# Splitting two query heads at once and moving 64-row blocks by DMA in a two-layer hybrid decoder step

## The chip, the cores and the metric

The kernel runs on one core of one Trainium2 chip. The metric is the device time of one execution in microseconds (us). A core has a matrix engine (TensorE, PE in the profile; its weight loads are shown apart as PEld), a vector engine (VectorE, DVE), an activation engine (ScalarE, ACT), a general engine (GpSimd, POOL) and SyncE (SP), whose queue issues all the transfers (DMAs) of this kernel. Each engine works through its own list of instructions in order and waits on semaphores for the others. Working data lies in SBUF (128 rows), results of matmuls in PSUM, inputs and outputs in device memory (DRAM).

## What is computed

One inference step over two layers with shared weights: 512 prompt tokens and 8 sample tokens (one for each of 8 sequences), 520 columns in all. Layer 1 is a gated linear recurrence with 16 heads of 128 (HGRN2). From the stream after it, one set of keys and values with 4 heads of 64 is made. Layer 2, the one that this change touches, is sliding-window attention with 32 query heads of 64, eight to a key head, and a sink logit for each head:

```python
HEAD_DIM = 64; N_Q_HEADS = 32; KV_HEADS = 4; WINDOW = 128; SEQ = 512; D_MODEL = 1024
kv = rmsnorm(h, kv_norm_g) @ w_kv
k_sh, v_sh = split(kv)
k_sh = rope_partial(k_sh.reshape(B, L, KV_HEADS, HEAD_DIM), pos)      # first 16 of 64 rotated
q, z = split(xn @ w_in_b)
q = rope_partial(q.reshape(B, L, N_Q_HEADS, HEAD_DIM), pos)
# in blocks of 128 queries, against the block before and their own:
s = einsum('bqhgd,bkhd->bhgqk', q, k) * HEAD_DIM ** -0.5
s = where(in_band, s, -inf)
pr = softmax(concat([s, sink]))[..., :-1]
o = einsum('bhgqk,bkhd->bqhgd', pr, v)
mix = (o.reshape(B, L, 2048) * silu(z)) @ w_out_b
h = h + rmsnorm(mix, post_norm_g); h = h + (p @ w_pe) * sigmoid(h @ w_pg)
```

## The kernel before

All activations lie transposed: 128 features in the rows, 520 tokens in the columns. Each operand of a matmul is split into a high part `hi`, a copy in the type `F32R`, and a low part `lo`, the rest. A projection tile (`Tile128`) is 128 output features: 8 chunks of the 1024 inputs, three products each (`hi*hi`, `lo*hi`, `hi*lo`), two halves of 260 columns, so 48 matmuls `pj<-xs,...` into a pair of PSUM banks. Weights come in transfers of 512 KB (`wr`, two buffers); ACT makes their high part `wh`, DVE or POOL the low part `wl` (four pieces of each are kept ahead).

Layer 2 has eight units (0 to 7) of four query heads. A unit is two query tiles, each with two heads of 64 rows, and two gate tiles. `query(c)` takes a query tile out of PSUM: `rope` is four vector operations (`tmp<-pj,ropeC`, a shuffle `tmp<-pj`, `tmp<-tmp,ropeS`, `tmp<-tmp,tmp`), and then for each of the two heads ACT writes the scaled high part into the head's 64 rows of a new tile `g`, and DVE the low part into the other 64 rows of the same tile. With 64 rows of high part above 64 rows of low part (or the other way round), one matmul over 128 rows does both products with a key tile that holds the same 64 rows twice. `keys_values` makes these key tiles `Kh` and `Kl` (in the profile `xr<-x`): the key's two parts are split once over 128 rows (`x`), and each head's 64 rows are then copied twice, `Kh` by ACT and `Kl` by DVE. The scores are the matmuls `ph<-xr,g`.

After that `block` runs once for each 128 queries of a unit: ACT copies the scores out (`b<-ph`), DVE puts the mask in (`b<-pmask,...`), takes the minimum (`an<-b`), ACT does four exponentials, one operation multiplies by the reciprocal (`b<-b,ad`), PE transposes (`ph<-ident,b`), ACT and DVE split the result (`g<-ph`, `g<-ph,g`), two multiplications mask it (`g<-g,tmask`), and PE applies the values (`ph<-g,b`, 512 columns). DVE adds the halves (`ao<-ph,m`), and at the unit's end multiplies by the gate and splits (`og`). `sample_b` does the attention of the sample tokens once for every four units; it clears its query tile `qs` with a POOL memset.

The output projection runs in groups: after unit 3's projections that of units 0 and 1, after unit 5's that of units 2 and 3, and so on (`GROUPS_B`).

The order of the instructions is not that of the code. Every operation is first only recorded by `Plan.enter`, with its dependencies and a cost from `price`. `Plan.issue` then goes through a modelled time and gives each engine what can start first; on PE, work beside the projections (attention) goes ahead of the next projection matmul as soon as it is ready. Operations recorded with `nc.either` go to DVE or, where DVE would not get to them soon, to POOL: `wl`, `b<-b,ad` and `g<-g,tmask` are such. Since all are issued by one helper, nearly every row of the profile has the line L164, and one goes by tiles' names. What comes out is a fixed order for each engine, with semaphores; the chip does not reorder it. The cost of a transfer in that model:

```python
t = max(t, lanes[0])
clock[e] = t + 0.45
pipe = max(pipe, t + 1.4) + cost       # cost: bytes / 3.3e5 us
op.end = pipe + 1.6
```

The functions that the diff touches, and what calls them:

Of the kernel before, what the change touches and what calls it, by code (L numbers as in the profile page):

```python
# [9 lines left out]
F32 = mybir.dt.float32  # L10
F32R = mybir.dt.float32r
I32 = mybir.dt.int32
AF = mybir.ActivationFunctionType
ALU = mybir.AluOpType
# [7 lines left out]
SEQ = 512  # L22
# [6 lines left out]
HD = 64  # L29
EPS = 1e-6  # L30
SCALE = HD ** -0.5
# [351 lines left out]
def half_of(x, half):  # L383
    return x[:, half * TH : (half + 1) * TH]


class Step:
# [647 lines left out]
    def keys_values(self, kvx):  # L1035
        nc = self.nc
        self.ks = [self.cp.tile([P, NB], F32, name=f"ks{n}") for n in range(2)]
        self.vs = self.cp.tile([NB, KVH * HD], F32, name="vs")

        def first():  # L1040
            if not self.Kh:
                self.Kh = [self.xr_(F32R, SEQ) for n in range(KVH)]
                self.Kl = [self.xr_(F32R, SEQ) for n in range(KVH)]

        def key(j):
            def evac(ps):
                k = self.x_()
                self.rope(ps, self.CR, self.SR, k)
                first()
                nc.sync.dma_start(self.o["ck"][j], k[:, SEQ - P : SEQ])  # L1050
                nc.sync.dma_start(self.o["ck_s"][j], k[:, SEQ:])
                nc.scalar.copy(self.ks[j], k[:, SEQ:])
                self.beside(lambda: twice(j, k))
            return evac

        def twice(j, k):
            hi, lo = self.split(k, self.x_)
            for a in range(2):
                n = 2 * j + a
                src = slice(a * HD, (a + 1) * HD)  # L1060
                for b in range(2):
                    dst = slice(b * HD, (b + 1) * HD)
                    nc.scalar.copy(self.Kh[n][dst], hi[src, :SEQ].bitcast(F32))
                    nc.vector.tensor_copy(self.Kl[n][dst], lo[src, :SEQ].bitcast(F32))

        def value(j):
            def evac(ps):
                v = self.x_()
                for h in range(2):
                    nc.vector.tensor_tensor(half_of(v, h), ps[:, h, :TH], half_of(self.R, h), op=ALU.mult)  # L1070
                if j == 0:
                    V = [self.small("b4", [P, 2, KVH, 2 * HD], 5, F32R) for n in range(2)]
                    self.V = [v[:, n] for v in V for n in range(2)] + [self.small("b2", [P, KVH, 2 * HD], 3, F32R)]
                pt = self.bank()
                for c in range(NCH):
                    nc.tensor.transpose(pt[:, c * P : (c + 1) * P], v[:, c * P : (c + 1) * P], self.ident)
                vt = self.tmp_(cols=SEQ)
                nc.scalar.copy(vt, pt)
                nc.sync.dma_start(self.o["cv"][:, j * P : (j + 1) * P], vt[:, SEQ - P :])
                rows = lambda c: vt[:, c * P : (c + 1) * P]  # L1080
                ds = self.tmp_(cols=3 * P)
                for n, c in ((0, 0), (2, 2), (1, 1), (3, 1), (4, 3)):
                    x = rows(c)
                    if n % 2 or n == 4:
                        d = ds[:, n // 2 * P : (n // 2 + 1) * P]
                        nc.either.tensor_tensor(d, x, rows(0 if n == 1 else 2), op=ALU.subtract)
                        x = d
                    x = x.rearrange("p (n d) -> p n d", n=2)
                    V = self.V[n][:, 2 * j : 2 * j + 2]
                    nc.scalar.copy(V[:, :, :HD], x)  # L1090
                    nc.either.tensor_tensor(V[:, :, HD:], x, V[:, :, :HD].bitcast(F32), op=ALU.subtract)
                p8 = self.bank()
                nc.tensor.transpose(p8[:NB, :P], v[:, SEQ:], self.ident)
                nc.scalar.copy(self.vs[:, j * P : (j + 1) * P], p8[:NB, :P])
                if j == 1:
                    nc.sync.dma_start(self.o["cv_s"], self.vs)
            return evac

        evs = ((2, value(0)), (3, value(1)), (0, key(0)), (1, key(1)))
        return [Tile128([(Weights(self.i["w_kv"][n]), 0)], KC, kvx, ev) for n, ev in evs]  # L1100

    def unit_proj(self, u, xs, st, done):

        nc = self.nc
        kvh = u // 2
        rows = slice((kvh % 2) * HD, (kvh % 2 + 1) * HD)
        st["Q"], st["z"], st["og"] = [], [], []

        def query(c):
            def evac(ps):  # L1110
                q = self.tmp_()
                self.rope(ps, self.C, self.S, q)
                for a in range(2):
                    s = self.g_(F32R)
                    me = slice(a * HD, (a + 1) * HD)
                    other = slice((1 - a) * HD, (2 - a) * HD)

                    nc.scalar.activation(s[me, :SEQ], q[me, :SEQ], AF.Copy, scale=-SCALE)
                    nc.vector.scalar_tensor_tensor(
                        s[other, :SEQ], q[me, :SEQ], -SCALE, s[me, :SEQ].bitcast(F32), op0=ALU.mult, op1=ALU.subtract  # L1120
                    )
                    st["Q"].append(s)
                    nc.scalar.copy(self.qs[rows, :, u % 4 * 4 + 2 * c + a], q[me, SEQ:])
                if c == 1 and u % 4 == 3:
                    self.beside(lambda: self.sample_b(u // 4), FIRST)
            return evac

        def gate(c):
            def evac(ps):
                t = self.tmp_()  # L1130
                nc.scalar.activation(self.two(t), self.flat(ps), AF.Tanh, scale=0.5)
                z = self.g_()
                nc.vector.scalar_tensor_tensor(
                    self.two(z), self.two(t), 1.0, self.flat(ps), op0=ALU.add, op1=ALU.mult
                )
                st["z"].append(z)
                if c == 0:
                    st["zs"] = self.small("zb", [P, 2, NB], 6)
                nc.scalar.copy(st["zs"][:, c], z[:, SEQ:])
                if c == 1:  # L1140
                    done()
            return evac

        def before():
            if u % 4 == 0:
                self.qs = self.small("qs", [P, NB, 16], 1)
                nc.gpsimd.memset(self.qs, 0.0)

        w = lambda n: [(Weights(self.i["w_in_b"][n]), 0)]
        return [Tile128(w(2 * u + c), KC, xs, query(c), before if c == 0 else None) for c in range(2)] + [  # L1150
            Tile128(w(16 + 2 * u + c), KC, xs, gate(c)) for c in range(2)
        ]
# [477 lines left out]
```

## Time and profile before

| | |
|---|---|
| Median of 3 runs | 1095.58 us (1094.31 to 1096.26) |
| The profiled execution | 1095.56 us, of which its span 1093.8 us |
| TensorE clock granted | 0.999 |
| PE / PEld / DVE / ACT / POOL busy | 98% / 97% / 85% / 64% / 11% of the span |
| DMA | 159.37 MB, 146 GB/s on average |

The span is the time from the first instruction to the last; the 1.8 us between it and the execution's time lie around it. Times in the rows below are us from the span's start, unless marked ns. A group's row ends in: busy time, mean ns of one | idle time of the engine just before them, and what ended it. A matmul's row is longer than the distance to the next, because matmuls are pipelined. The keys and values are projected in the stretch up to about 675 us, the eight units' projections with their attention and the output projection run from there to about 1030 us, and the rest is the residual, the norm and the per-layer gate.

### The profile page before, as it was taken

The numbers are of one execution on the slowest core, as the hardware profiler recorded it, in microseconds if no ns is written. First come the engines' busy times: TensorE is split into PE (matmuls) and PEld (weight loads), VectorE is DVE, ScalarE is ACT, GpSimd is POOL, SyncE is SP. The second block draws the span as 40 slices with busy tenths as digits, with TensorE's granted clock in tenths as the row PEclk, the third lists the DMA queues.
The fourth block names the chain that finished last, engine by engine and source line by source line (L and its number), as shares of the span: only waits on it lengthen the run. The fifth ranks groups of instructions, "written<-read, shape, count | busy, mean of one in ns | idle before, by whom it ended". The sixth has DMA issues, their size and how long they took to land.

```text
span 1093.8 us, 23692 instructions
## 1 busy us (share of the span) xinstructions
PE 1073.2 (98%) x8831; PEld 1058.5 (97%) x8831; DVE 924.3 (85%) x1986; ACT 700.9 (64%) x1849; POOL 125.4 (11%) x209
## 2 busy tenths in 40 slices
PE   7999999999999999999999999999999999999998
PEld 6999999999999999999999999999999999999998
DVE  7898888758789588888879989999986997999883
ACT  7787667557775576777636656776674773774551
POOL 1211121011220112121101000111110000000000
PEclk9999999999999999999999999999999999999999
DMA  8555767556666566677655442221213122214433
GB/s 275 174 194 170 195 178 210 147 170 211 168 202 177 154 203 191 194 204 212 200 156 172 133 144 83 75 86 59 83 54 96 59 78 97 78 62 147 144 102 93
DMA packets 148427, 159.37 MB, mean 146 GB/s; under 512 B 100308, under 2 KB 107356, under 8 KB 148312
## 3 DMA queue, kind: packets, MB, share of 16 engines
q1 hardware_dynamic: 148312, 157.85, 47.5%
q8 instruction: 70, 1.15, 0.4%
q14 instruction: 45, 0.37, 0.1%
HBM read 130.03 MB, written 27.78 MB: 144 GB/s over the span
## 4 chain that ended last, share of the span: by engine, by line
PE 72%; DVE 13%; DMA 5%; ACT 5%; issue 3%; SPq 2%; POOL 0%; POOLq 0%; DVEq 0%; ACTq 0%
PE pj L164 59%; PE ph L164 13%; DVE tmp L164 3%; DVE g L164 2%; SPq L164 2%; DMA xr<-td 2%; DVE wl L164 2%; DVE b L164 1%; DVE ao L164 1%; DVE xr L164 1%; ACT b L164 1%; DVE acc L164 1%; ACT g L164 1%; DVE og L164 1%; ACT wh L164 1%
## 5 line engine op out<-in xcount | busy, mean ns | idle before, releaser
L164 PE MATMUL pj<-xs,wh 128*128 128x260 f32 x3328 | 569.4, 285 | 0.9 <-ACT xs L164 0.7
L164 PEld LDWEIGHTS pj<-xs,wh 128*128 128x128 f32 x3328 | 469.4, 189 | 4.4 <-ACT xs L164 1.9
L164 PE MATMUL pj<-xs,wl 128*128 128x260 f32 x1664 | 348.2, 285 | 0.0
L164 PEld LDWEIGHTS pj<-xs,wl 128*128 128x128 f32 x1664 | 260.7, 188 | 0.6
L164 ACT CAST wh<-wr 128x512 fp32r<-128x512 f32 x288 | 177.3, 619 | 121.8 <-PE pj L164 110.4
L164 DVE TENSOR_TENSOR wl<-wr,wh 128x512 fp32r<-128x512 f32 x274 | 187.7, 688 | 54.0 <-ACT wh L164 53.4
L164 PE MATMUL pj<-og,wh 128*128 128x260 f32 x1056 | 184.9, 285 | 0.7 <-ACT g L164 0.5
L164 PEld LDWEIGHTS pj<-og,wh 128*128 128x128 f32 x1056 | 151.6, 188 | 2.5 <-ACT g L164 0.7
L164 PE MATMUL pj<-og,wl 128*128 128x260 f32 x512 | 107.9, 285 | 0.0
L164 ACT ACTIVATE tmp<-pj 128x520 f32<-128x520 f32 (+1 forms) x93 | 48.0, 528 | 53.9 <-PE pj L164 53.4
L164 PEld LDWEIGHTS pj<-og,wl 128*128 128x128 f32 x512 | 80.9, 189 | 0.5
L164 ACT ACTIVATE sb<-sb,g 128x128 f32<-128x128 f32 x128 | 65.0, 558 | 0.8 <-DVE sb L164 0.8
L164 ACT ACTIVATE sb<-sb,nv 128x128 f32<-128x128 f32 x128 | 63.2, 560 | 0.2
L164 DVE TENSOR_TENSOR x<-x,pj 128x520 f32<-128x520 f32 (+1 forms) x80 | 46.5, 584 | 16.1 <-PE pj L164 15.2
L164 ACT ACTIVATE b<-b,an 128x129 f32<-128x129 f32 x128 | 50.8, 400 | 5.5 <-DVE an L164 5.4
L164 PE MATMUL pj<-xs,b 128*128 128x260 f32 x384 | 52.1, 284 | 0.9 <-ACT tmp L164 0.5
L164 DVE TENSOR_TENSOR g<-g,b 128x256 f32<-128x256 f32 x96 | 40.6, 423 | 12.1 <-PE ph L164 9.9
L164 PE MATMUL ph<-xr,b 128*128 128x128 f32 x320 | 49.3, 275 | 0.4 <-ACT b L164 0.3
L164 DVE COPY_PREDICATED xr<-lmask,ph 128x256 f32<-128x256 int32 x96 | 47.0, 490 | 3.1 <-PE ph L164 2.8
L164 PEld LDWEIGHTS pj<-xs,b 128*128 128x128 f32 x384 | 48.2, 188 | 1.4 <-ACT tmp L164 0.7
L164 ACT COPY b<-g 128x256 f32<-128x256 f32 (+1 forms) x112 | 40.8, 374 | 10.7 <-DVE g L164 9.2
L164 PE MATMUL ph<-g,b 128*128 128x512 f32 x112 | 43.8, 404 | 2.5 <-DVE g L164 2.3
(201 smaller groups left out, 1709.3 us busy)
## 6 DMA issues: line engine op xcount, KB each, us to landing
wr<-in_w_in_a SPq DMA_DIRECT2D x64, 512.0 KB, 4.4
sb<-sd SPq DMA_DIRECT2D x32, 512.0 KB, 5.3
wr<-in_w_in_b SPq DMA_DIRECT2D x32, 512.0 KB, 3.4
td<-tmp SPq DMA_DIRECT2D x42, 256.0 KB, 2.5
xr<-td SPq DMA_DIRECT2D x168, 64.0 KB, 3.6
sb<-in_state SPq DMA_DIRECT2D x16, 512.0 KB, 5.8
out_st_s<-sb SPq DMA_DIRECT2D x16, 512.0 KB, 3.4
wr<-in_w_out_a SPq DMA_DIRECT2D x16, 512.0 KB, 3.7
```

Source lines behind the costliest of these rows:

```text
L164: op = Op(len(self.ops), self.level, on, [lambda c=c: c(*a, **k) for c in calls], [self.price(e, name, ins, a, k) for e in on], on[0] == " ...
```

## The change

In `query`, the scaling and the split are done once for a whole query tile: `hi` gets both heads' high parts in 128 rows, `lo` both heads' low parts. Head 0's tile needs its low part below its high part, head 1's its high part above its low part; so the lower 64 rows of `hi` and the upper 64 rows of `lo` change places. This is done by four transfers of 128 KB through a DRAM tile `qd`: both blocks are written to it (`qd<-g`), and both are read back crosswise (`g<-qd`). In `keys_values`, the sixteen copies of 64 rows become sixteen transfers from SBUF to SBUF.

```diff
@@ keys_values, twice
                 for b in range(2):
                     dst = slice(b * HD, (b + 1) * HD)
-                    nc.scalar.copy(self.Kh[n][dst], hi[src, :SEQ].bitcast(F32))
-                    nc.vector.tensor_copy(self.Kl[n][dst], lo[src, :SEQ].bitcast(F32))
+                    for to, x in ((self.Kh[n], hi), (self.Kl[n], lo)):
+                        nc.sync.dma_start(to[dst].bitcast(F32), x[src, :SEQ].bitcast(F32))
@@ unit_proj, query
                 q = self.tmp_()
                 self.rope(ps, self.C, self.S, q)
+                hi, lo = self.g_(F32R), self.g_(F32R)
+
+                nc.scalar.activation(hi[:, :SEQ], q[:, :SEQ], AF.Copy, scale=-SCALE)
+                nc.vector.scalar_tensor_tensor(
+                    lo[:, :SEQ], q[:, :SEQ], -SCALE, hi[:, :SEQ].bitcast(F32), op0=ALU.mult, op1=ALU.subtract
+                )
+
+                d = self.plan.tile(self.dp, [2, HD, SEQ], F32, self.name("qd"), "qd", 3)
+                ends = hi[HD:, :SEQ].bitcast(F32), lo[:HD, :SEQ].bitcast(F32)
+                for n in range(2):
+                    nc.sync.dma_start(d[n], ends[n])
+                for n in range(2):
+                    nc.sync.dma_start(ends[n], d[1 - n])
+                st["Q"].extend((hi, lo))
                 for a in range(2):
-                    s = self.g_(F32R)
                     me = slice(a * HD, (a + 1) * HD)
-                    other = slice((1 - a) * HD, (2 - a) * HD)
-
-                    nc.scalar.activation(s[me, :SEQ], q[me, :SEQ], AF.Copy, scale=-SCALE)
-                    nc.vector.scalar_tensor_tensor(
-                        s[other, :SEQ], q[me, :SEQ], -SCALE, s[me, :SEQ].bitcast(F32), op0=ALU.mult, op1=ALU.subtract
-                    )
-                    st["Q"].append(s)
                     nc.scalar.copy(self.qs[rows, :, u % 4 * 4 + 2 * c + a], q[me, SEQ:])
```

What the planner makes of it differs from the keys on, on every engine. In the rows below a tile's name carries its number.

POOL, from the last row of the norm ahead of the units to the clearing of the sample attention's tile `qs` behind unit 3's queries. Before:

```order
L164 TENSOR_TENSOR wl_1848<-wr_1840,wh_1847 128x512
L164 TENSOR_TENSOR g_1885<-g_1883,tmask 128x512
L164 TENSOR_TENSOR g_1897<-g_1895,tmask 128x512
L164 TENSOR_TENSOR b_1857_1953<-b_1857_1953,ad_1957 128x4x128
L164 TENSOR_TENSOR g_1962<-g_1960,tmask 128x512
L164 TENSOR_TENSOR g_1973<-g_1971,tmask 128x512
L164 TENSOR_TENSOR g_1985<-g_1983,tmask 128x512
L164 TENSOR_TENSOR b_1935_2031<-b_1935_2031,ad_2035 128x4x128
L164 TENSOR_TENSOR g_2049<-g_2047,tmask 128x512
L164 TENSOR_TENSOR g_2061<-g_2059,tmask 128x512
L164 TENSOR_TENSOR g_2073<-g_2071,tmask 128x512
L164 MEMSET qs_2226 128x128
```

And changed:

```order
L164 TENSOR_TENSOR wl_1931<-wr_1921,wh_1930 128x512
L164 TENSOR_TENSOR wl_2010<-wr_2000,wh_2009 128x512
L164 TENSOR_TENSOR wl_2021<-wr_2011,wh_2020 128x512
L164 TENSOR_TENSOR wl_2100<-wr_2090,wh_2099 128x512
L164 TENSOR_TENSOR g_2055<-g_2053,tmask 128x512
L164 MEMSET qs_2234 128x128
```

Eleven operations of POOL become five here; the other six stand on DVE. Behind the memset POOL has 7 before and 9 now, without those of the norms.

PE, unit 0's first scores (`xr` are the key tiles, `g_1825` and `g_1826` what the first query tile left). Before:

```order
L164 MATMUL pj_1837<-xs_1732,wh_1821 128x260 x2
L164 MATMUL pj_1837<-xs_1733,wh_1828 128x260 x2
L164 MATMUL pj_1837<-xs_1733,wl_1829 128x260 x2
L164 MATMUL pj_1837<-xs_1734,wh_1828 128x260
L164 MATMUL ph_1856<-xr_1796,g_1825 128x128
L164 MATMUL ph_1856<-xr_1800,g_1825 128x128
```

And changed:

```order
L164 MATMUL pj_1907<-xs_1730,wh_1843 128x260 x2
L164 MATMUL pj_1907<-xs_1731,wh_1843 128x260 x2
L164 MATMUL pj_1907<-xs_1731,wl_1844 128x260
L164 MATMUL ph_1858<-xr_1796,g_1825 128x128
L164 MATMUL ph_1858<-xr_1800,g_1825 128x128
```

The first scores stood inside unit 0's first gate tile (`pj_1837`) and now stand inside unit 1's first query tile (`pj_1907`). Between a query tile's last matmul and the first score that reads it, PE had 49 to 85 matmuls over the eight units, and now has 125 to 152.

SP, the end of the keys' transfers and unit 0's queries, changed (before, only the loads `wr` stood here):

```order
L164 DMA xr_1803<-x_1815 64x512
L164 DMA qd_1827<-g_1825 64x512
L164 DMA wr_1851<-in_w_in_b 128x1024
L164 DMA qd_1838<-g_1836 64x512
L164 DMA qd_1827<-g_1826 64x512
L164 DMA wr_1910<-in_w_in_b 128x1024
L164 DMA qd_1838<-g_1837 64x512
L164 DMA g_1825<-qd_1827 64x512
L164 DMA g_1826<-qd_1827 64x512
L164 DMA g_1836<-qd_1838 64x512
L164 DMA g_1837<-qd_1838 64x512
L164 DMA wr_1921<-in_w_in_b 128x1024
```

SP's list grows by 80 transfers (32 `qd<-g`, 32 `g<-qd`, 16 `xr<-x`). The four blocks that are read back wait for the landing of those that were written, and the weight load `wr_1921` stands behind them.

## The prediction

> **What bounds the kernel now.** I read the page's first part, then the busy time in stretches, then what PE waits for, and then the timeline around those waits.
>
> ```profile
> span 1093.8 us, 23692 instructions
> PE 1073.2 (98%) x8831; PEld 1058.5 (97%) x8831; DVE 924.3 (85%) x1986; ACT 700.9 (64%) x1849; POOL 125.4 (11%) x209
> core 0: us, PE busy (x) PEld busy (x) DVE busy (x) ACT busy (x) POOL busy (x), PEclk, DMA share, GB/s
> 685.00:785.00 100.00, 96.96 (x762) 93.26 (x761) 97.37 (x184) 69.67 (x220) 14.43 (x10) 1.00 0.23 75
> 785.00:840.00 55.00, 54.37 (x437) 53.14 (x437) 43.25 (x99) 34.91 (x110) 5.93 (x5) 1.00 0.21 69
> 840.00:962.00 122.00, 122.00 (x988) 120.12 (x987) 111.72 (x213) 77.10 (x233) 3.28 (x2) 1.00 0.25 83
> 962.00:1030.00 68.00, 68.00 (x557) 67.12 (x555) 60.59 (x135) 38.16 (x114) 2.72 (x3) 1.00 0.36 122
> ```
>
> PE is busy nearly everywhere, and the change takes no matmul away. All that it touches lies between the keys (from about 665 us) and 1030 us; the order ahead of that is the same. From 840 to 1030 us PE has no idle time at all, although DVE is busy for 91% of it. Only from 685 to about 800 us, where the first units' attention runs, do PE and DVE contend: DVE is busy for 97 of 100 us there, and PE stops now and then. What PE waits for from 680 to 800 us:
>
> ```profile
> PE ph L164 <- DVE g L164: 2.3, 3, 1.1
> PE ph L164 <- DVE b L164: 0.6, 1, 0.6
> PE ph L164 <- DVE tmp L164: 0.5, 1, 0.5
> ```
>
> These 3.4 us in five waits are what is to be had, and a little more, as the largest shows in PE's timeline:
>
> ```profile
> 710.59 0.40 PE L164 MATMUL pj<-xs,wl 128*128 128x260 f32 x2
> 710.83 0.28 PE L164 MATMUL pj<-xs,wh 128*128 128x260 f32 x1
> 712.17 0.74 PE L164 MATMUL ph<-g,b 128*128 128x512 f32 x2 [1.06 <-DVE g L164]
> 1072.34 17.39 PE pj L164 x143
> ```
>
> A matmul's row lasts 0.28 us, but in an unbroken run (the last row, of the chain of waits) 143 of them take 17.39 us, 0.12 each. So each wait costs 0.16 us more than its row says (here 1.34 from start to start, less 0.12, is 1.22, shown as 1.06). Five waits: 3.4 + 5 x 0.16 = 4.2 us. That is 0.4% of the time, and the most that this change can win where the profile shows it.
>
> Why PE waited for DVE there, in DVE's and POOL's timelines:
>
> ```profile
> 708.70 1.81 DVE L164 TENSOR_TENSOR tmp<-tmp,ropeS 128x520 f32<-128x520 f32 x1
> 711.42 0.69 DVE L164 TENSOR_TENSOR g<-ph,g 128x512 fp32r<-128x512 f32 x1
> 748.47 1.78 DVE L164 TENSOR_TENSOR tmp<-tmp,ropeS 128x520 f32<-128x520 f32 x1
> 774.28 1.81 DVE L164 TENSOR_TENSOR tmp<-tmp,ropeS 128x520 f32<-128x520 f32 x1
> 708.34 1.61 POOL L164 TENSOR_TENSOR g<-g,tmask 128x512 fp32r<-128x512 f32 x1 [16.30 <-ACT g L164]
> 748.31 1.39 POOL L164 TENSOR_TENSOR g<-g,tmask 128x512 fp32r<-128x512 f32 x1 [7.46 <-ACT g L164]
> 774.03 1.50 POOL L164 TENSOR_TENSOR g<-g,tmask 128x512 fp32r<-128x512 f32 x1 [0.95 <-ACT g L164]
> 796.73 1.30 POOL L164 TENSOR_TENSOR wl<-wr,wh 128x512 fp32r<-128x512 f32 x1 [4.78 <-ACT wh L164]
> 796.82 1.30 DVE L164 TENSOR_SCALAR tmp<-tmp,bd 128x128 f32<-128x128 f32 x1
> L164 DVE TENSOR_TENSOR tmp<-tmp,ropeS x16: 684/698/1814, 681.2 to 963.1; 128x520 f32<-128x520 f32 x16
> ```
>
> The last row says that this multiplication takes 0.70 us (median of 16). Three times it took 1.8, each time because POOL had begun an operation 0.16 to 0.36 us before; the `g<-ph,g` behind it, for which PE waited, came 1.1 us later. So all three `DVE g` waits follow a collision of DVE with POOL, and the `DVE tmp` wait follows one with a `wl` on POOL (1.30 us for 128 columns).
>
> **The change part by part.** Rows of before that price it (in the 685 to 785 us stretch, then over the span):
>
> ```profile
> L164 DVE SCALAR_TENSOR_TENSOR g<-tmp,g 64x512 fp32r<-64x512 f32 x14 | 9.6, 685 | 0.4
> L164 DVE CAST xr<-x 64x512 fp32r<-64x512 f32 x4 | 1.7, 422 | 0.1
> L164 DVE TENSOR_TENSOR g<-g,tmask 128x512 fp32r<-128x512 f32 x9 | 6.2, 684 | 0.0
> L164 DVE SCALAR_TENSOR_TENSOR ao<-ao,g 128x512 f32<-128x512 f32 x16 | 10.4, 684 | 0.1
> L164 ACT ACTIVATE g<-tmp 64x512 fp32r<-64x512 f32 x32 | 20.2, 630 | 10.8 <-DVE tmp L164 10.4
> ```
>
> Queries on DVE: an operation's length goes by its columns, not its rows (64x512 at 685 ns, 128x512 at 684). So two become one: 14 in the stretch become 7, 7 x 0.685 = 4.8 us less. Over the span, 16 x 0.685 = 11.0.
>
> Keys' copies on DVE: 4 fall away in the stretch, 1.7 us, and 4 shortly before, another 1.7, for which PE did not wait.
>
> Given back: six operations that POOL did there stand on DVE now, 6 x 0.684 = 4.1 us. So DVE's work in the stretch falls by 4.8 + 1.7 - 4.1 = 2.4 us of 97.4. The collisions matter as much: POOL has 5 operations there instead of 11, so in proportion 3 x 5/11 = 1.4 collisions instead of 3; 1.6 x 1.1 = 1.8 us less. In all 4.2 us less for DVE, which chances to be all that PE waited. Whether `wl` on POOL, which is 4 of the 5, holds up ropeS as `g<-g,tmask` did isn't in the trace; the row at 796.73 shows it for another DVE operation, so I count it. If it did not, one `g<-g,tmask` of 8 would be left, 0.4 collisions. The Trainium skill (SBUF — State Buffer, Who interferes with whom) speaks against that milder count: a vector instruction with two SBUF inputs contends with any GpSimd instruction that reads SBUF, and the one that started first holds the shared ports to its end. By it the sum is the one below; by the milder count it would be 0.3 us more gain.
>
> I do not take all of it. Wait by wait: the three `DVE g` waits are 2.3 + 3 x 0.16 = 2.8 us; with 1.6 of 3 collisions gone and DVE a little freer I take three quarters, 2.1. The `DVE tmp` wait (0.66) sits in the sample attention's chain behind another POOL operation; a POOL operation stands near that place still: half, 0.3. The `DVE b` wait (0.76) is in the first block's softmax, behind the load of the exponential's table on ACT, which stays:
>
> ```profile
> 693.83 1.28 ACT L164 ACT_TABLE_LOAD   x1
> ```
>
> 0 for it. Sum of the gains 2.4 us. Bounds: 0 and 4.2.
>
> ACT: 16 x 0.63 = 10 us less for the queries, and the keys' 8 copies. ACT is busy for 70% of the stretch and none of PE's waits names it: 0. If DVE were no longer late, PE would be next, not ACT.
>
> PE: the same matmuls, the scores later. Each unit's attention moves back by the longer path of its queries, and ends before its group's output projection: the last unit's last value matmuls stand some 110 matmuls, 13 us, ahead of the first one that reads their result, and in between lie a few DVE and ACT rows of 0.4 to 0.7 us each. 0; without that cover it would cost what the next paragraph gives.
>
> Transfers of the queries. The trace has no copy of 64 rows to DRAM and back, so I bound it with these rows:
>
> ```profile
> 706.85 0.69 DVE L164 TENSOR_TENSOR tmp<-pj,ropeC 128x520 f32<-128x520 f32 x1
> 707.46 0.75 DVE L164 STREAM_SHUFFLE tmp<-pj 128x520 f32<-128x520 f32 x1
> 708.11 0.67 DVE L164 TENSOR_TENSOR wl<-wr,wh 128x512 fp32r<-128x512 f32 x1
> td<-tmp SPq DMA_DIRECT2D x42, 256.0 KB, 2.5
> og<-hd SPq DMA_DIRECT2D x8, 260.0 KB, 3.9
> L164 SPq DMA_DIRECT2D xr<-td x168: 557/627/1559, 47.4 to 548.0; - x168
> DMA to landing us min/median/max: 2.0/3.5/7.6
> ```
>
> From the end of a query tile: ropeC 0.69, shuffle 0.75, a `wl` between 0.67, ropeS 0.70, the sum 0.69, ACT 0.63, DVE 0.68, so 4.8 us. Then two writes (2.5 us to land, as the `td` writes; issue 0.6 each) and two reads (3.9, as the `og` reads from DRAM; 0.6 each): 2.5 + 3.9 + 4 x 0.6 = 8.8. Together 13.6 us. PE has at least 125 matmuls of 0.12 us in between, 15.0. So it is hidden, with 1.4 us to spare: 0. Bounds: the landing rows' range (2.0 to 7.6) gives 2.0 + 2.0 + 2.4 = 6.4 to 2 x 7.6 + 2.4 = 17.6 us for this leg, 3.8 less or 7.4 more than the cover of 15.0 - 4.8 = 10.2; a gain is excluded, since nothing waits for earlier queries, so 0 to 7.4 lost.
>
> Keys' transfers: 16 of 128 KB from SBUF to SBUF, 16 x 0.6 = 9.6 us of SP at most; the first scores stand 145 to 152 matmuls, 17 us, behind the first unit's queries, of which the keys are ahead. 0. The queries' 64 add 64 x 0.6 = 38 us of issue over 300 us, and all 80 move 10.5 MB in a stretch where the DMA engines are 21 to 36% busy (the stretches above): 0.
>
> Weight loads wait in the same queue behind the transfers. From 690 to 1000 us, ACT's wait and the loads' rows:
>
> ```profile
> ACT wh L164 <- PE pj L164: 35.6, 27, 2.3
> L164 SPq DMA_DIRECT2D wr<-in_w_in_b x26: 327/328/328, 692.1 to 946.8; - x26
> DMA to landing us min/median/max: 3.3/3.4/4.5
> ```
>
> ACT's split of the weights waits for PE to free a piece, so the weights are there before they are wanted; a load lands in 3.4 us and there are 26 in 255 us. A load held up for 5 us would be covered by the pieces that are split already: four of them, the product of 4 x 24 matmuls x 0.12 = 11.5 us. 0, up to 3 us if several are held.
>
> **Sum.** -2.4 us. The profiled execution took 1095.56 us (span 1093.8 and 1.8 around it), 0.02 under the median of 1095.58. So 1093.2 us, a gain of 0.22%.
>
> **Rivals.** *Nothing to be seen.* Collisions depend on where POOL's operations fall. Over the whole of layer 2 POOL has 18 such operations before (4 collided) and 14 now; in proportion 3.1 of 4 stay, and the waits only move: (2.8 + 0.66) x 0.9/4 = 0.8 us, 1094.8. For it: DVE's net relief is 2.4 us of 97, and PE's share of 97 to 98% leaves nothing to win elsewhere. Against it: from 840 us on DVE is as full and PE does not wait. The Trainium skill (Perfetto Trace Analysis, Identifying the Most-Contended Engine) says to optimize the engine with the highest occupancy first, judging TensorE by its weight loads' share; that is PE with 97%, and the change takes nothing from PE; by that rule the time stays, 1095.6.
>
> *The round trip isn't hidden.* If write and read together take longer than the cover of 10.2 us less issue, which is 7.8 us for both landings, PE stops at the scores. Once it has stopped, PE is late against all the rest, so later units lose less. With landings of 5.5 us each: 3.2 us at the first, as much again over the others, less 1.2 for waits that this swallows: +5, 1100.6. For it: landings up to 7.6 us occur. Against it: those have 128-byte pieces and share the queue with 0.5 MB loads; in this stretch the DMA is 23% busy.
>
> *All of it.* Every one of the five waits goes: 1091.4. For it: both DVE's work and collisions fall by as much as PE waited. Against it: the table load.
>
> **How the numbers follow.** What can be told from no change here is about 0.2%, 2.2 us. The forecast has 0.54: its own range, 1 to 4 us of gain, is 1091.6 to 1094.6, and somewhat more than half of it (0.30) lies beyond 2.2 us. All of it has 0.14, nothing to be seen 0.17, the round trip or held loads together 0.15. So faster 0.30 + 0.14 = 0.44, same 0.24 + 0.17 = 0.41, slower 0.15. The range reaches from 1090.9, all the waits and half a microsecond of small ones, to 1097.5, where the slower cases begin; it leaves out those and a little below, under 2 in 10.
>
> **What would show it.** In the changed profile: 16 `g<-tmp,g` of 128x512 at 0.69 us; DVE about 12 us less busy; of the waits of PE for `DVE g` about one left; ropeS over 1 us once or twice; no wait of PE for `DMA g<-qd` or `DMA xr<-x`; landings of `g<-qd` under 4 us; ACT's `wh` waiting for PE, not for `wr`. I am wrong if PE waits for `DMA g<-qd`, or if the collisions come back on other rows.

## The result, and the profile after

The changed kernel took 1090.01 us (median of 4 runs, 1089.13 to 1091.30), beside 1094.94 us (4 runs, 1094.07 to 1096.26) for the kernel before: 4.9 us less, ratio 0.9950 with a 95% interval of 0.9937 to 0.9962. Measured once more beside experiments it was 0.9940 (0.9927 to 0.9952). I had forecast 1093.2 us, in a range from 1090.9 to 1097.5. The sign was right, but the gain was twice the forecast, and the time came out below the range.

The first part of the page after, and the busy time in the stretches that were shown of before (columns: stretch, its length, PE, PEld, DVE, ACT, POOL, granted clock, DMA share, GB/s):

```profile
span 1087.9 us, 23796 instructions
PE 1071.9 (99%) x8831; PEld 1058.7 (97%) x8831; DVE 906.0 (83%) x1966; ACT 688.6 (63%) x1825; POOL 115.8 (11%) x205
```

```profile
685.00:785.00 100.00, 99.73 (x808) 97.73 (x807) 89.86 (x178) 68.34 (x213) 6.97 (x6) 1.00 0.41 121
785.00:840.00 55.00, 55.00 (x443) 54.00 (x443) 46.55 (x108) 35.85 (x114) 1.29 (x1) 1.00 0.25 80
840.00:962.00 122.00, 122.00 (x991) 120.06 (x990) 101.53 (x194) 72.94 (x223) 7.97 (x7) 1.00 0.38 113
```

From 685 to 785 us PE now gets through 808 matmuls instead of 762, and DVE is busy for 90 of 100 us instead of 97. After 840 us both kernels run at the same pace (988 and 991 matmuls in 122 us): nearly all of the gain is made by then.

What PE waited for from 660 to 1030 us, and DVE's multiplication with `ropeS`, which collided three times before:

```profile
PE pj L164 <- DVE x L164: 0.5, 1, 0.5
PE ph L164 <- DVE ad L164: 0.2, 1, 0.2
```

```profile
L164 DVE TENSOR_TENSOR tmp<-tmp,ropeS x16: 690/694/704, 680.6 to 954.2; 128x520 f32<-128x520 f32 x16
```

Of the five waits only one is left, 0.2 us ahead of the first block's transposes at 708 us (the wait for `x` belongs to the residual at 1026 us and was there before). The longest of the 16 `ropeS` operations takes 0.704 us: no collision at all.

The new transfers, in the list of DMA issues (KB each, median us from issue to landing) and by tile:

```profile
qd<-g SPq DMA_DIRECT2D x32, 128.0 KB, 2.3
g<-qd SPq DMA_DIRECT2D x32, 128.0 KB, 3.6
xr<-x SPq DMA_DIRECT2D x16, 128.0 KB, 3.3
```

```profile
L164 SPq DMA_DIRECT2D qd<-g x32: 445/467/1454, 684.0 to 959.1; - x32
L164 SPq DMA_DIRECT2D g<-qd x32: 444/541/1206, 691.9 to 965.6; - x32
```

No wait of PE names them. The two ends of the stretch that the change touches are marked by the same three matmuls of the norms ahead and behind (before, then after):

```profile
L164 PE MATMUL ph<-ident,rsr x3: 270/271/272, 642.7 to 642.9; 128*128 128x128 f32 x3
L164 PE MATMUL ph<-ident,rsr x3: 272/272/273, 1031.5 to 1031.8; 128*128 128x128 f32 x3
```

```profile
L164 PE MATMUL ph<-ident,rsr x3: 270/271/272, 643.6 to 643.8; 128*128 128x128 f32 x3
L164 PE MATMUL ph<-ident,rsr x3: 271/272/276, 1026.1 to 1026.3; 128*128 128x128 f32 x3
```

From mark to mark it is 388.9 us before and 382.5 us after, 6.4 us less; 0.9 us of it is lost ahead of the stretch, where the programs are alike. This length (the "stretch" below) is read for every kernel, from its one profiled execution. It can differ from the gain over all runs: in the profiled execution of e7 below, 1.7 us were won ahead of the stretch, where the programs are alike.

### The profile page after: what moved, and what is told of

Same layout as the page of the kernel before. It is cut to its first block, busy times and chain, and to the rows that moved or that the text cites. A ratio compares the mean times of both kernels' runs of the same rounds, so it can differ in the third digit from the quotient of the medians.

```text
span 1087.9 us, 23796 instructions
## 1 busy us (share of the span) xinstructions
PE 1071.9 (99%) x8831; PEld 1058.7 (97%) x8831; DVE 906.0 (83%) x1966; ACT 688.6 (63%) x1825; POOL 115.8 (11%) x205
## 4 chain that ended last, share of the span: by engine, by line
PE 81%; DVE 5%; DMA 5%; ACT 4%; SPq 3%; issue 2%; POOL 0%; DVEq 0%; ACTq 0%
PE pj L164 66%; PE ph L164 15%; SPq L164 3%; DMA xr<-td 2%; DMA wr<-in_w_in_a 1%; DVE tmp L164 1%; DVE xr L164 1%; DVE wl L164 1%; ACT g L164 1%; DVE acc L164 1%; ACT wh L164 1%; DMA td<-tmp 1%; ACT tmp L164 1%; ACT sb L164 0%; ACT og L164 0%
## 5 line engine op out<-in xcount | busy, mean ns | idle before, releaser
L164 POOL TENSOR_TENSOR wl<-wr,wh 128x512 fp32r<-128x512 f32 x15 | 19.6, 1309 | 260.6 <-ACT wh L164 241.4
```

Of the source, the lines that this page charges most:

```text
L164: op = Op(len(self.ops), self.level, on, [lambda c=c: c(*a, **k) for c in calls], [self.price(e, name, ins, a, k) for e in on], on[0] == " ...
```

## The experiments

Eighteen kernels, in groups of two to four that shared their runs of the kernel before. The theories in the expectations: **A**, what wins is that DVE has less work (the queries' halved operations); **B**, that the scores come later, which gives the attention's chain slack; **C**, that POOL and DVE collide less, or more widely, that POOL's operations fall in better places; **E**, that relief or late scores alone are enough; **K**, that the keys' part is a large part. "Matmuls" after a query tile are those of PE between the tile's last one and the first score that reads it.

All results together. Gain is 1 minus the ratio, with its interval; the stretch is that of the profiled execution; collisions are DVE operations from 660 to 805 us that overlap one of POOL and took over 0.25 us longer than the median of the same operation over all these kernels (their number, and the us they lost), counted in DVE's timeline.

| Kernel | gain % (interval) | stretch us | collisions |
|---|---|---|---|
| before | 0 | 388.9 | 4, 4.4 |
| the change | 0.50 (0.38 to 0.63); 0.60 (0.48 to 0.73) | 382.5; 382.7 | 0 |
| e1 keys | 0.12 (0.01 to 0.23) | 388.0 | 3, 2.7 |
| e2 queries (relief + late) | 0.25 (0.15 to 0.34) | 385.9 | 2, 1.6 |
| e3 late + keys | 0.52 (0.36 to 0.67) | 383.5 | 0 |
| e4 relief + keys | 0.47 (0.31 to 0.63) | 383.4 | 0 |
| e9 late | 0.47 (0.33 to 0.60) | 383.6 | 0 |
| e10 relief | 0.40 (0.28 to 0.53) | 385.3 | 2, 2.1 |
| e5 before, no POOL | -0.10 (-0.19 to -0.01) | 390.5 | 0 |
| e17 late, no POOL | -0.60 (-0.79 to -0.42) | 394.0 | 0 |
| e18 relief, no POOL | 0.47 (0.34 to 0.61) | 383.6 | 0 |
| e7 queries, no POOL | 0.12 (0.03 to 0.20) | 389.4 | 0 |
| e6 the change, no POOL | 0.39 (0.27 to 0.52) | 383.7 | 0 |
| e8 direct transfers | 0.27 (0.18 to 0.36) | 385.1 | 0 |
| e11 change, more DVE | 0.03 (-0.06 to 0.12) | 387.3 | 2, 1.6 |
| e13 before, four moved | 0.24 (0.15 to 0.33) | 386.9 | 0 |
| e14 change, POOL as before | -0.21 (-0.32 to -0.10) | 390.7 | 8, 4.3 |
| e15 late, POOL as before | -0.23 (-0.33 to -0.12) | 391.2 | 7, 5.4 |
| e16 queries, four moved | 0.21 (0.10 to 0.31) | 386.6 | 0 |

**The parts of the change.** e1 keeps the old `query`; e2 keeps the keys' copies. e3 makes the parts head by head again, so that DVE has its work back but the scores stay late; e4 leaves the transfers of the queries' parts out, so that DVE has the relief and the scores are early.

```diff
 e3, in query
-                nc.scalar.activation(hi[:, :SEQ], q[:, :SEQ], AF.Copy, scale=-SCALE)
-                nc.vector.scalar_tensor_tensor(lo[:, :SEQ], q[:, :SEQ], -SCALE, hi[:, :SEQ]...)
+                for a in range(2):
+                    me = slice(a * HD, (a + 1) * HD)
+                    nc.scalar.activation(hi[me, :SEQ], q[me, :SEQ], AF.Copy, scale=-SCALE)
+                    nc.vector.scalar_tensor_tensor(lo[me, :SEQ], q[me, :SEQ], -SCALE, hi[me, :SEQ]...)
 e4, in query
-                for n in range(2):
-                    nc.sync.dma_start(d[n], ends[n])
-                for n in range(2):
-                    nc.sync.dma_start(ends[n], d[1 - n])
```

> Keys' parts by transfers, queries as before. Three theories of the 4.9 us that the change won. Theory A, less work for DVE: the queries' halved operations are most of it (11.0 of the 18 us that DVE has less); of the keys' copies 1.7 us lie in the stretch where PE waits: 0.5 to 1.5 us faster than before. Theory B, later scores: here the scores stand as early as before (49 to 99 matmuls behind a tile's last), so 0 to 0.5 us. Theory C, collisions of POOL with DVE: POOL has 4 of g<-g,tmask, one b and one ropeS ahead of the memset of qs, against 11 operations before and 5 after; if the collisions are what costs, those left decide: 1 to 3 us.

> Queries in one operation for two heads and exchanged by transfers, keys' copies as before. Theory A (less work for DVE): 3.5 to 4.9 us faster than before. Theory B (later scores, 124 to 177 matmuls here): 4.5 to 5 us, all of it. Theory C (collisions): POOL has six operations ahead of the memset of qs, none of them ropeS; 3 to 5 us. If the keys' copies were what made PE wait, under 1.5 us.

> The change, but the parts are made head by head again, in two operations of 64 rows on ACT and on DVE, and then exchanged by transfers: the scores are as late as in the change (138 to 170 matmuls behind a tile's last), and DVE has the queries' 11 us back. Theory A (less work for DVE): 1 to 2.5 us faster than before, and PE waits for DVE g between 690 and 790 us again. Theory B (later scores): 4 to 5 us faster, no such waits. Theory C (collisions): by how many of POOL's seven operations ahead of the memset of qs meet a DVE operation.

> The change without the four transfers of the queries' parts; what is left out is the exchange of the blocks, so that the scores are of mixed-up parts, with the same matmuls. DVE has the relief, and the scores are as early as before (41 to 69 matmuls). Theory A (less work for DVE): 4 to 5 us faster than before. Theory B (later scores): 0 to 1.5 us faster, with PE waits for DVE g left, of 0.5 us and more. Theory C: POOL has a wl, a ropeS of its own, two g<-g,tmask and another wl ahead of the memset of qs; few collisions, 3 to 5 us.

Measured: 0.12, 0.25, 0.52 and 0.47%, so 1.3, 2.7, 5.7 and 5.2 us. Neither A nor B came out: late scores without relief (e3) won as much as the change, and nearly as much did relief without late scores (e4), but both together without the keys' part (e2) only half. In e2 the largest wait is behind another collision (DVE's and PE's timelines; POOL's `b<-b,ad` began at 734.44 us):

```profile
734.52 1.51 DVE L164 TENSOR_TENSOR og<-ao,og 128x512 fp32r<-128x512 f32 x1
737.74 0.63 PE L164 MATMUL ph<-ident,b 128*128 128x128 f32 x4 [0.85 <-DVE b L164]
```

**Without POOL.** In layer 2 the operations that the planner may give to either engine go to DVE alone. Then no collision is left, and DVE has 14 or 18 operations more.

```diff
 e5 on before, e6 on the change, e7 on e2
-        nc.either.tensor_tensor(lo, raw, hi.bitcast(F32), op=ALU.subtract)
+        (nc.vector if self.Kh else nc.either).tensor_tensor(lo, raw, hi.bitcast(F32), op=ALU.subtract)
 ... and the same for b<-b,ad, g<-g,tmask and ropeS
 e8, in query of the change
-                d = ...; two writes to d, two reads back
+                top, low = self.g_(F32R), self.g_(F32R)
+                for n, (to, x, y) in enumerate(((top, hi, lo), (low, hi, lo))):
+                    src = slice(n * HD, (n + 1) * HD)
+                    nc.sync.dma_start(to[:HD, :SEQ].bitcast(F32), x[src, :SEQ].bitcast(F32))
+                    nc.sync.dma_start(to[HD:, :SEQ].bitcast(F32), y[src, :SEQ].bitcast(F32))
```

> The kernel before, but in layer 2 the four kinds of operation that the planner may give to DVE or POOL (wl, ropeS, b<-b,ad, g<-g,tmask) all go to DVE: nothing of POOL's can meet DVE there, and DVE has 18 operations, about 12 us, more, 11 of them ahead of 790 us. Theory C (collisions with POOL, and POOL's longer operations, make PE wait): 2 to 4.5 us faster than before, no DVE operation over its usual length. Theory A (DVE has too much work while the first units run): 2 to 6 us slower, more PE waits for DVE between 690 and 800 us.

> The change, with the same four kinds of operation on DVE alone in layer 2: 14 operations, about 9.5 us, more for DVE, 5 of them ahead of 785 us. Theory C (collisions): as the change or up to 0.5 us faster, 5 to 6 us faster than before. Theory A (DVE's work): the relief of some 11 us is taken back, 1 to 3 us slower than the change; if the relief is more than PE needs, no difference.

> Only the queries' part of the change (keys' copies as before), again with the four kinds on DVE alone in layer 2. The queries' part with the planner's choice won 2.7 us and showed PE waits behind b<-b,ad on POOL. Theory C (where POOL's operations fell made the difference to the whole change): 4.5 to 6 us faster than before. The rival, that the keys' eight copies on DVE and ACT are themselves worth 2 us: 2 to 3 us.

> The change, but the queries' blocks go from SBUF to SBUF in four direct transfers into two further tiles in place of two writes to DRAM and two reads back. Of the round trip's 2.3 + 3.6 us to landing, the second half falls away. If the round trip is hidden, as I said: as the change within 0.3 us, 4.5 to 5.5 us faster than before. If a part of it is still paid, in PE steps too short to show: 1 to 2 us faster than the change.

Measured: e5 0.10% slower, e6 0.39% faster, e7 0.12% faster, e8 0.27% faster. e5 came out as neither theory said. Of the 2.9 us that PE waited between 685 and 785 us only 0.6 are left, but waits come back at the sample attention, because DVE, with 18 operations more, is late there; and there the granted clock falls too (the stretches from 685 to 840 us):

```profile
685.00:785.00 100.00, 99.28 (x793) 96.63 (x792) 96.29 (x186) 68.40 (x207) 0.20 (x1) 1.00 0.25 80
785.00:840.00 55.00, 52.16 (x400) 49.88 (x399) 46.59 (x109) 37.61 (x122) 0.00 (x0) 0.97 0.17 58
```

793 matmuls instead of 762 in the first stretch, but 400 instead of 437 in the second. e6 shows that the change keeps two thirds to four fifths of its gain with nothing on POOL (0.39 of 0.60 or 0.50%).

e8 won 2.5 to 3.6 us less than the change although a direct transfer lands in 2.6 us. The planner, for which one transfer is shorter than two, put the scores earlier, and the first eight transfers, among the keys' own, landed late (PE's timeline and the DMA view up to 692 us):

```profile
693.82 1.42 PE L164 MATMUL ph<-xr,g 128*128 128x128 f32 x8 [1.37 <-DMA g<-g]
```

```profile
L164 SPq DMA_DIRECT2D g<-g x8: 462/568/893, 684.8 to 691.9; - x8
DMA to landing us min/median/max: 5.0/5.3/6.3
```

PE was ready for them at 692.45 us; in the change the first score starts at 696.54 us. This wait is the largest part of e8's loss that the profile shows. So the round trip is hidden, but only because the planner leaves it that much room.

**One part alone, and the reverse.** e9 is e3 with the keys' copies of before: late scores alone. e10 is e4 with them: relief alone. e11 does the change's subtraction three times over (`for _ in range(3):` around it). e12 is the change again.

> As the kernel with two operations of 64 rows and late scores, but the keys' parts are copied by ACT and DVE as before: neither the queries' nor the keys' relief of DVE, only the later scores (138 to 170 matmuls). Theory E (either is enough: PE's stops need a full DVE and early scores at once): 4.5 to 5.7 us faster than before. Theory K (the keys' part is worth 2 to 3 us beside either): 2.5 to 3.5 us faster. If only the relief counted: 0 to 1 us.

> The queries' parts in one operation for two heads, without the exchange (which leaves the four transfers out, so that the scores are of mixed-up parts, with the same matmuls), and keys' copies as before: the queries' relief of DVE alone, with early scores (41 to 65 matmuls). Theory E: 4 to 5.2 us faster than before. Theory K: 2 to 3 us faster. If only the delay counted: 0 to 1 us; but the run with the keys' transfers speaks against that.

> The change, with the subtraction of each query tile done three times over (the same result each time): 32 more operations of 0.684 us on DVE, 22 us, twice what the change took from the queries. Theory E (late scores alone are enough): PE has slack enough, 4 to 5 us faster than before, DVE at 95 of 100 us in the stretch from 685 to 785 us, waits of PE under 1 us there. If the relief is what wins: 0 to 2 us faster than before, or slower, with PE waits for DVE of 2 us and more.

> The change itself, beside the others on the same chip: 4.9 us faster than before by the first measurement, 4.3 to 5.7 us here. It gives the figure that the parts are held against.

Measured: 0.47, 0.40, 0.03 and 0.60%. Beside one part alone K fell: without the keys' part late scores and relief win nearly as much as with it (0.47 against 0.52, 0.40 against 0.47). Beside both it did not: e2 and the change differ by the keys' part alone, and by 0.25 to 0.35%; so do e7 and e6, without POOL, by 0.27%. How much of this is the keys' part itself is open, since e2 has two collisions where the change has none, and e7's clock falls (below). E seemed to be right, but e11 speaks against it: with 22 us of additional work for DVE the whole gain was gone, late scores or not. This isn't DVE's work alone, though, for the planner also gave POOL ten operations between 685 and 805 us where the change has seven, and two collided. One of its waits shows, too, that `wl` on POOL holds up DVE, which I had left open (e11, POOL, DVE and PE):

```profile
740.32 1.60 POOL L164 TENSOR_TENSOR wl<-wr,wh 128x512 fp32r<-128x512 f32 x1 [2.60 <-ACT wh L164]
740.69 1.78 DVE L164 TENSOR_TENSOR og<-ao,og 128x512 fp32r<-128x512 f32 x1
742.39 0.68 DVE L164 TENSOR_TENSOR g<-ph,g 128x512 fp32r<-128x512 f32 x1
743.12 0.50 PE L164 MATMUL ph<-g,b 128*128 128x512 f32 x1 [1.01 <-DVE g L164]
```

And e9's success had another suspect: its planner had given POOL 15 operations, none of which collided.

**POOL's operations moved, all else in place.** Here the planner runs as it did, and only at the issue are listed operations given to the other engine, so that the rows of PE, ACT and SP stay word for word those of the kernel named.

```diff
 in Plan.issue
+        two = [op for op in self.ops if len(op.on) > 1]
...
-            self.tc.keep_in_program_order(op.calls[n]())
+            m = 1 - n if len(op.on) > 1 and two.index(op) in SWITCHED else n
+            self.tc.keep_in_program_order(op.calls[m]())
```

> The kernel before, in its own order on PE, ACT and SP; only the four operations of POOL that met DVE (three g<-g,tmask and one wl) are issued on DVE in the same place of the program. DVE gets 4 x 0.684 = 2.7 us of work and loses 3.8 us of collisions. Theory C (the collisions are what PE waits for): the three waits for DVE g and the one for tmp go, 2.5 to 3.5 us faster than before. Theory E (DVE's whole backlog, or early scores): the backlog changes by 1.1 us, 0 to 1.2 us faster, the waits move to other rows.

> The change in its own order, but in layer 2 exactly those operations stand on POOL that stood there before (18 in place of 14, 13 of them ahead of 815 us). Theory C: collisions come back, two to four by the rate of before (4 of 18), each worth about 1.2 us: 2.4 to 4.8 us of the gain are lost again. Theory E: relief and late scores leave slack for them: as the change or at most 1 us slower.

> Late scores alone (two operations of 64 rows, keys' copies), again with POOL's operations of the kernel before and no other order. Theory C: 2.4 to 4.8 us slower than the late scores with their own choice, so 0 to 2 us faster than before. Theory E (late scores give slack): 3.5 to 5 us faster than before.

> The queries' part alone in its own order, with four operations moved from POOL to DVE: three b<-b,ad, behind which PE waited at 711 and 736 us, and a wl that met DVE. Theory C, in its wider form (POOL's operations are slower and collide): the waits of 0.9 and 0.3 us go, 4 to 5 us faster than before. If the keys' part is what is missing: 2.5 to 3 us faster, as it was.

Measured: e13 0.24% faster (2.6 us), e14 0.21% and e15 0.23% slower, e16 0.21% faster. E falls: with POOL's operations of before, late scores turn from 5.2 us faster to 2.5 us slower, and the change from 4.9 faster to 2.3 slower. e13 took the four collisions away for 2.7 us of work that DVE got instead, and won 2.6 us net, the lower part of C's expectation. The wait for `tmp` went; the three for `DVE g`, which C had go as well, only shrank, from 2.3 to 1.3 us. The waits that stay, from 680 to 800 us:

```profile
PE ph L164 <- DVE g L164: 1.3, 3, 0.6
PE ph L164 <- DVE b L164: 0.6, 1, 0.6
```

e15 shows a collision with its price (POOL, DVE and PE). PE's matmul starts as the held-up operation ends, at 724.12 us:

```profile
722.29 1.29 POOL L164 TENSOR_TENSOR g<-g,tmask 128x512 fp32r<-128x512 f32 x1 [31.46 <-DVE ao L164]
722.32 1.80 DVE L164 TENSOR_TENSOR g<-g,tmask 128x512 fp32r<-128x512 f32 x1
724.04 0.68 DVE L164 TENSOR_TENSOR g<-ph,g 128x512 fp32r<-128x512 f32 x1
724.17 0.50 PE L164 MATMUL ph<-g,b 128*128 128x512 f32 x1 [0.95 <-DVE g L164]
```

e14 and e15 lost more than C foresaw for two to four collisions. They had eight and seven, and waits also where there was none, up to 970 us; from 680 to 1000 us PE waited in e14

```profile
PE ph L164 <- DVE b L164: 2.2, 6, 0.6
PE ph L164 <- DVE g L164: 2.1, 6, 0.6
```

so these two also show what 26 or 27 operations cost in places that the planner had not foreseen, and are no price for collisions alone. e16 went against C: off POOL the `b<-b,ad` at 711 us stood behind other work in DVE's queue, and the wait grew from 0.28 to 1.66 us. To move an operation off POOL helps only where DVE has room.

**The square without POOL.** Late scores alone and relief alone, e9 and e10 with the edit of e5: no choice of POOL and no collision is left.

> Late scores alone (two operations of 64 rows, keys' copies), and in layer 2 wl, ropeS, b<-b,ad and g<-g,tmask on DVE alone, so that nothing of POOL's matters. The kernel before in that form was 1.1 us slower than before. If late scores are worth something by themselves: 3 to 4 us faster than before. If they only changed the planner's choice for POOL: as the kernel before in that form, 0 to 2 us slower than before, with DVE as full.

> The queries' parts in one operation for two heads alone (the exchange left out, so that the scores are of mixed-up parts, with the same matmuls; keys' copies as before), and the same four kinds of operation on DVE alone in layer 2. DVE has the queries' 11 us less. If relief is worth something by itself: 3 to 4.3 us faster than before. If it only changed the planner's choice for POOL: 0 to 2 us slower than before.

Measured: late scores 0.60% slower, relief 0.47% faster. Beside e5 (0.10% slower) and e7 (0.12% faster, both parts): without POOL relief wins, 0.57% by itself (e5 to e18) and 0.72% beside late scores (e17 to e7), and late scores lose, 0.50 and 0.35%. Late scores won in e3 and e9 only with the places that the planner gave POOL's operations there. Relief alone with POOL's operations of before was not run; the change, which has it, lost there (e14). Part of what e17 and e7 lose is the clock (e17's stretches, then e18's):

```profile
685.00:785.00 100.00, 99.71 (x807) 97.75 (x806) 93.78 (x182) 68.95 (x202) 0.20 (x1) 1.00 0.38 114
785.00:840.00 55.00, 52.36 (x377) 48.24 (x376) 47.66 (x111) 38.14 (x129) 0.00 (x0) 0.94 0.23 73
962.00:1030.00 68.00, 67.39 (x522) 64.57 (x521) 65.26 (x141) 39.62 (x123) 0.00 (x0) 0.97 0.42 137
```

```profile
685.00:785.00 100.00, 99.79 (x802) 97.66 (x801) 97.90 (x194) 68.39 (x220) 0.00 (x0) 1.00 0.24 80
785.00:840.00 55.00, 54.80 (x445) 53.74 (x445) 43.62 (x101) 35.54 (x111) 0.20 (x1) 1.00 0.20 68
```

The clock takes 55 x 0.06 + 68 x 0.03 = 5.3 us of e17's stretch; by the same sum 1.7 us of e5's and, at 0.94 from 785 to 840 us, 3.3 us of e7's. Without that the stretches are 388.8 (neither), 388.7 (late), 383.6 (relief) and 386.1 us (both): relief 2.6 to 5.2 us, late scores between nothing and 2.5 us lost. The first stretch is not where relief shows. With nothing on POOL all four kernels gain there: 793 (neither), 807 (late), 802 (relief) and 799 matmuls (both) instead of 762, although DVE in e18 is as busy as before, 97.9 of 100 us. Relief shows at the sample attention, from 785 to 840 us: 400, 377, 445 and 404 matmuls, where the kernel before has 437 and the change 443 (the clock explains some 14 of the missing ones in e5 and 27 in e17 and e7).

So two things are at work. In the first stretch POOL's operations cost PE: of the 46 matmuls that the change gains there, e5 gains 31 by their removal, with the order that the planner then makes. And with POOL's work on DVE as well, PE stops at the sample attention, in e7 too; e18 keeps its pace there, and so does e6 (441 matmuls), where the keys' part stands beside the other two. The change has both, fewer operations on POOL, none of which meets one of DVE, and less work for DVE. How its gain divides between them isn't shown.

## Where the prediction was right and where it failed

**What bounds the kernel.** Right. All that PE waited for in the stretch was DVE, and the gain came from there: 46 more matmuls by 785 us, and 55 more by 962 us (2242 instead of 2187 from 685 us on, by the stretches), at 0.12 us each 6.6 us, close to the 6.4 us by which the stretch is shorter.

**The cap of 4.2 us.** This step failed first. I added the five waits and 0.16 us for each and called it the most that could be won. By the views shown the waits fell from 4.2 to 0.4 us (0.2 and one 0.16), 3.8 us; the stretch fell by 6.4. Read from start to start, the stretch has the same 3,103 matmuls in both kernels, and the steps that are at least 0.12 us longer than usual for their kind held up PE for 5.2 us in ten places before and 0.6 us in two after. So another 0.8 us were in places with less than about 0.3 us each, which the view of the waits doesn't list; the row ahead, 0.16 us longer than the distance to the next, covers most of such a wait. The remaining 1.8 us lie in steps nearer to the usual, where short waits can't be told from large and small matmuls in another order; they stay open. The count of matmuls has it all, and that was in the view I quoted: 762 in 100 us against 988 in 122, where with 8.10 a microsecond it would have been 810, at 0.12 us each 5.8 us.

**Collisions by proportion.** The second failed step. I let 1.4 of 3 stay, since 5 of 11 operations stay on POOL; none stayed. A proportion was no basis: what remained on POOL was mostly `wl` (4 of the 5), and whether an operation meets DVE depends on its place to within a few tenths of a microsecond. The profiled kernels had from 0 to 8: the change has 7 operations on POOL between 685 and 805 us and no collision, e14 has 13 and eight. The price on DVE, 1.1 us, was right (1.0 to 1.1 us for the four of before). What one costs PE by itself isn't shown: e13 won 2.6 us without the four, but with 2.7 us more work for DVE. And that each `DVE g` wait follows a collision was true, but the collision was not all of its cause, since 1.3 of the 2.3 us stayed in e13.

**Three quarters, half, none.** From 4.2 us I took 2.4 by fractions for each wait. These were too small: of the 4.0 us between 2.4 and the 6.4 measured in the stretch, 1.4 are listed waits that I let stay, and 2.6 lie beyond the cap. The wait for `b` behind the table load, for which I took nothing, went from 0.6 to 0.2 us, and that for `tmp` went altogether. *All of it*, the rival at 1091.4 us with a chance of 0.14, came nearest to 1090.0.

**The queries on DVE.** Right in kind and size: 16 `g<-tmp,g` of 128 rows, in the changed stretch

```profile
L164 DVE SCALAR_TENSOR_TENSOR g<-tmp,g 128x512 fp32r<-128x512 f32 x7 | 4.8, 684 | 0.0
```

7 where there were 14 of 685 ns. Over the span DVE fell by 18.3 us, not by "about 12". I had left the collisions (4.4 us) and most of the keys' copies out of that figure. With 11.0 for the queries, 3.4 for the keys and 2.7 given back for four operations from POOL the sum is 16.1; DVE's rows added up one by one fall by 16.3. The other 2.0 of the 18.3 are rows that overlap, which the busy time counts once. Without POOL this relief is the one part that wins by itself (e18 against e5); that it is what the change wins by in its own form isn't shown.

**The keys.** Nothing, I said. With the planner's own choice e1 gives 0.12%, and beside late scores or relief alone they add 0.05 and 0.07%, less than the intervals. But the change wins 0.25 to 0.35% more than e2, and e6 0.27% more than e7, and the keys' part is all that differs: some 3 us for a term that I had put at nothing. Part of it goes by collisions (e2) and the clock (e7), and the rest is open.

**The round trip.** Right: 2.3 and 3.6 us to land for 2.5 and 3.9, 0.47 and 0.54 us to issue for 0.6, and hidden. The rival that it isn't hidden is real at another place: e8 paid 1.4 us where PE came to the scores 4 us earlier.

**Nothing to be seen.** Its argument, that PE at 97 to 98% leaves nothing to win, failed: the busy share hid the short waits. The rule of the Trainium skill that I set beside it (Perfetto Trace Analysis, Identifying the Most-Contended Engine) says which engine to work on first; that the time would therefore stay was my inference from it. It fell by 0.5% with PE's weight loads at 97% before and after: the work on DVE was what PE waited for.

Open: why the two parts together without the keys' part won less than relief alone, with POOL (e2, 0.25%) and without it (e7, 0.12%). e2's collision at 734 us and the longer way of `b` over POOL stand in its profile, but e16, which removed both, was no faster.

## What to carry to other kernels

Where a matrix engine looks 98% busy, count its instructions in equal stretches and compare with a stretch that runs free; a list of waits leaves out the short ones. Where two engines share work by a planner's choice, an edit that changes a few operations deals all the collisions anew: before a part of it is credited, run it with that choice taken away, and with the old choice put back. A part that wins only with one deal (late scores: 0.47% faster, 0.60% slower without POOL) can't be credited with the gain. And parts of a change need not add up: two that win 0.4 to 0.5% each won 0.25% together.

## What I had not expected of the hardware

The granted clock can fall to half without PE being idle for long. It did so in four places of the kernels above, once in e5, once in e7 and twice in e17, for 3.4 or 6.8 us. In e7 it fell at 794.95 us: PE waited 0.2 and 0.4 us and then ran sixteen small matmuls of the sample attention, 16 columns each (stretches of 4 us, and PE's timeline):

```profile
792.00:796.00 4.00, 3.34 (x19) 2.64 (x19) 3.96 (x9) 1.32 (x5) 0.00 (x0) 0.87 0.42 131
796.00:800.00 4.00, 4.00 (x17) 3.81 (x18) 2.28 (x9) 2.62 (x13) 0.00 (x0) 0.50 0.02 6
```

```profile
794.16 2.70 PE L164 MATMUL ph<-tmp,b 128*128 128x16 f32 x16
797.69 0.42 PE L164 MATMUL pj<-og,wh 128*128 128x260 f32 x1
797.91 0.42 PE L164 MATMUL pj<-og,wl 128*128 128x260 f32 x1
```

The step between the last two is 0.22 us instead of 0.12. The Trainium skill (TensorE: Matmul & The Clock Gate, Part 1: The HAM clock gate) has the clock at half after an idle window of about 3.4 us; the half clock agrees with the step here, but no window of that length was idle. Few matmuls alone are not the reason: 11 of them in the 3.4 us from 792.62 us in e17, and a wait of 1.66 us in e16, passed at the full clock. Such a row of sixteen small matmuls stands in each of the 20 profiles four times. The clock fell behind the four rows that had 0.6 us or more of PE waits in the 5 us ahead of them, and behind none of the 76 others, which had at most 0.5 us. No run was made to test this. Where the clock falls, a short stall costs more behind it than the stall itself: by the half clock's length about 3.4 us in e7, behind waits of 0.6 us.
